# Row fetch for 96 tokens instead of 80, and 17 instead of 10 homes for expert tables

## The chip, the core and the metric

The kernel runs on one core of a Trainium2 chip. The metric is the device time of one execution in microseconds, median over runs. The engines that matter here are TensorE (PE, with its weight loads PEld), VectorE (DVE), ScalarE (ACT), GpSimd (POOL) and the two DMA queues that SyncE (SP) and GpSimd feed. All numbers of the trace come from one profiled execution.

## What is computed

Two transformer blocks on 256 tokens of width 1024. The change is in the last part of the second block, a layer of 16384 experts from which each token uses 128 (8 heads, 16 each):

```python
def peer_ffn(h, w_pq, peer_keys, peer_u, peer_v):
    q = (ht @ w_pq).reshape(T, PEER_HEADS, 2, PEER_HALF)
    sub = jnp.einsum('thpc,hpnc->thpn', q, peer_keys)
    s_top, i_top = lax.top_k(sub, PEER_TOPK)
    ...
    best_s, pos = lax.top_k(cand_s, PEER_TOPK)
    expert = jnp.take_along_axis(cand_i, pos, axis=-1)
    gate = jax.nn.softmax(best_s, axis=-1)
    def chunk(args):
        xc, ec, gc = args
        u = jnp.take(peer_u, ec, axis=0)
        act = jax.nn.gelu(jnp.einsum('cd,ckd->ck', xc, u))
        vv = jnp.take(peer_v, ec, axis=0)
        return jnp.einsum('ck,ckd->cd', gc * act, vv)
```

`peer_u` and `peer_v` are 16384 x 1024 in float32. The result is added to x, which is then normed and stored.

## The kernel before

**Two paths for the expert layer.** The 256 tokens are divided. For the last 176 tokens (N = 256 - TS) the kernel works densely: it multiplies with all 16384 rows of both tables and lets a matrix of gates (zero for experts that were not chosen) select. For the first 80 tokens (TS) it works sparsely: it fetches only the rows that these tokens chose, 128 rows of 4 KB per fetch.

**Dense path.** Each table comes as 128 tiles of 128 x 1024 float32, 512 KB each, by SP's DMA queue (`_dma`, L192). TensorE does 8 matmuls (16 passes in the trace) per tile. First all 128 tiles of u (L1580, then gelu on ACT and a product on DVE, L1598), with 22 batches of gate matmuls between them (`g_batch`, L1536); then all 128 tiles of v (L1659), which add up in four PSUM banks `acc`. The first 24 u tiles (U0) need no gates. The first gate batch needs the top-k of the second half of the tokens, which DVE works out. After the last v tile the sums in `acc` are scaled into `fT`: four of the eight parts on DVE (L1665), four on ACT (L1663).

**Sparse path.** `sparse` fetches with an indirect DMA from GpSimd (L1484) into one of four buffers `ug` (SB = 4). DVE consumes each: a dot product per u row (L1489, 80 of them), then a weighted sum per v row into `sacc` (L1501 and twice L1499, 80 of them). The fetch that uses a buffer again waits for DVE's instruction on it. At the end TensorE adds `sacc` up over partitions (L1676) and DVE scales the result into the sparse columns of `fT` (L1680). Then `back` turns `fT` around (L1650), adds x, norms and stores.

**Homes.** A table tile needs a place in SBUF when its load is issued. Before, ten 4 KB-per-partition places are used in turn: four of the pool `raw`, three each of `whi` and `wlo`. `self.depth` says how many tiles ahead of its use a load may be issued. The tiles of weights that come before the tables (`w_pq` last) use the same queue and the same `raw` places. The tags `bighi` and `biglo` hold `h4`, the input of the routing, which is dead once `hN` and the routing products are made.

**What sets the order.** Each engine takes its instructions from one queue in a fixed order. The program order is `peer()`; a scheduler of the framework reorders it at build time by a simulated time line, so where an instruction stands in its engine's queue follows from that schedule and not from the source alone. The source spreads the steps of `sparse` over the tiles (`step`, SC = 222).

Of the kernel before, what the change touches and what calls it, by code (L numbers as in the profile page):

```python
# [9 lines left out]
F32 = mybir.dt.float32  # L10
# [122 lines left out]
class Kernel:  # L133
# [47 lines left out]
    PRE = (0, 0, 4)  # L181
    DQ = "gpsimd"

    def _dma(self):
        n = self.ndma - self.nwide
        if n < 0 or n % 10 < 4:
            t = self.raw.tile([128, 1024], F32, name="raw")
        elif n % 2 == 0:
            t = self.his.tile([128, 1024], F32, name="raw", tag="whi")
        else:  # L190
            t = self.los.tile([128, 1024], F32, name="raw", tag="wlo")
        self.nc.sync.dma_start(t, self.wspec[self.ndma][0])  # L192
        self.rawt[self.ndma] = t
        self.ndma += 1
# [5 lines left out]

    def _split(self, pin=lambda i: i):
        j = self.nsplit
        while self.ndma < min(len(self.wspec), j + self.depth):
            self._dma()
        t = self.rawt.pop(j)
        flag = self.wspec[j][1]
        if "R" in flag:
            self.wt[j] = t
            self.nsplit += 1
            return  # L210
        if "G" in flag:
            self.nc.gpsimd.tensor_tensor(t, t, self.gt1, OP.mult)
        late = "L" in flag
        hi = (self.late if late else self.his).tile([128, 1024], F32R, name="whi")
        lo = (self.late if late else self.los).tile([128, 1024], F32R, name="wlo")
        i = self.nc.scalar.activation(hi, t, AF.Copy)  # L216
        pin(i)
        if self.fenced:
            self.behind(i, self.fence[0])
        e = self.nc.gpsimd if j in self.POOL_LO or "P" in flag else self.nc.vector  # L220
        i = e.tensor_tensor(lo, t, hi.bitcast(F32), OP.subtract)  # L221
        pin(i)
        if self.fenced:
            self.fenced -= 1
            if e is self.nc.vector:
                self.behind(i, self.fence[1])
        self.wt[j] = (hi, lo)
        self.nsplit += 1
# [1212 lines left out]
                V.tensor_tensor(self.gb[1][:, t0], g, self.gb[0][:, t0], OP.subtract)  # L1441


    TG = ((0, 64), (64, 16))
    TS = 80
    SB = 4

    def rows_init(self, SP):
        nc, V = self.nc, self.nc.vector
        TS, self.SP = self.TS, SP  # L1450
        m = [SP.tile([128, 1024], F32, name="ug", bufs=self.SB) for _ in range(3)]
        for t, i in zip(m, (4, 3)):
            self.dq.dma_start(t[0:TS], self.modd[:, 1024 * i:1024 * i + 1024].to_broadcast([TS, 1024]))
        h = m[2][0:TS]
        V.scalar_tensor_tensor(h, self.x[0:TS, 0], self.r4[0:TS], m[0][0:TS], op0=OP.mult, op1=OP.mult)
        V.tensor_tensor(h, h, m[1][0:TS], OP.add)
        self.hrow, self.pair = [], []
        for t0, n in self.TG:
            r = SP.tile([128, 1024], F32, name=f"hrow{t0}")
# [5 lines left out]
            self.pair.append(p)  # L1465
        self.slot = SP.tile([128, 2, TS], F32, name="slot")
        self.sdot, self.sw = [SP.tile([128, TS], F32, name=n) for n in ("sdot", "sw")]

    def slots(self, e, i, j):
# [4 lines left out]
        V.tensor_copy(ids[0:TS, 1], fl(e)[0:TS])  # L1474
        for t0, n in self.TG:
            for q in range(128 // n):
                self.dq.dma_start(self.slot[n * q:n * q + n, :, t0:t0 + n], ids[t0:t0 + n, :, n * q:n * q + n])

    def sparse(self):
        nc, V, A, G = self.nc, self.nc.vector, self.nc.scalar, self.nc.gpsimd  # L1480

        def fetch(rows, s):
            t = self.SP.tile([128, 1024], F32, name="ug", bufs=self.SB)
            G.indirect_dma_start(t, None, rows, bass.IndirectOffsetOnAxis(self.slot[:, 0, s:s + 1].bitcast(U32), 0))  # L1484
            return t
        slots = [(g, s) for g, (t0, n) in enumerate(self.TG) for s in range(t0, t0 + n)]
        for g, s in slots:
# [6 lines left out]
        for g, s in slots:  # L1494
            t = fetch(self.io["peer_v"].rearrange("a b c -> (a b) c"), s)
            w = self.sw[:, s:s + 1]
            if s == self.TG[g][0]:
                self.sacc.append(self.SP2.tile([128, 1024], F32, name=f"sacc{g}"))
# [50 lines left out]
    def peer(self):  # L1549
        nc, V, A, G, tc = self.nc, self.nc.vector, self.nc.scalar, self.nc.gpsimd, self.tc  # L1550
# [17 lines left out]
        with ExitStack() as st:  # L1568
# [4 lines left out]
            TS, N = self.TS, 256 - self.TS  # L1573
# [3 lines left out]
            def u_dot(ps):  # L1577
                w = self.wget_raw()
                for k in range(8):
                    nc.tensor.matmul(ps, w[:, 128 * k:128 * k + 128], hN[:, k], start=k == 0, stop=k == 7)  # L1580
            A0 = st.enter_context(tc.tile_pool(name="act0", bufs=1))
            act = [A0.tile([128, self.U0, N], F32, name="act0")]
            at = lambda i: act[0][:, i] if i < self.U0 else act[1][:, i - self.U0]

            def u_chunk(i):
                ps = self.psum()
                u_dot(ps[:, 0:N])
                A.activation(at(i), ps[:, 0:N], AF.Gelu_apprx_tanh)

            def u_mul(i, n, U):  # L1590
                ps = self.psum()
                u_dot(ps[:, 0:N])
                w = at(i)
                t = U.tile([128, N], F32, name="ut")
                A.activation(t[:, 0:n], ps[:, 0:n], AF.Gelu_apprx_tanh)  # L1595
                if n < N:
                    A.activation(w[:, n:], ps[:, n:N], AF.Gelu_apprx_tanh)
                V.tensor_tensor(w[:, 0:n], w[:, 0:n], t[:, 0:n], OP.mult)  # L1598
            with tc.tile_pool(name="route", bufs=1) as K:
                R = type("R", (), dict(iota=iota, pool=PT))  # L1600
                with self.ps_pool("prt") as self.prt:
                    subs = self.route(R, K, h)
                with self.ps_pool("ptk") as self.ptk:
                    self.topk(R, K, subs)
                self.depth = 10
                for i in range(self.U0):
                    u_chunk(i)
            self.ls.close()
# [47 lines left out]
            for i in range(128):  # L1656
# [12 lines left out]
                if i == 126:  # L1669
                    for _ in sparse:  # L1670
                        pass
                    for d0 in (0, 4):
                        ps = self.psum()
                        for d in range(4):
                            for g, (t0, n) in enumerate(self.TG):
                                nc.tensor.matmul(ps[:, TS * d + t0:TS * d + t0 + n],  # L1676
# [69 lines left out]
```

## Time and profile before

| | |
|---|---|
| median of 3 runs | 1355.09 us (1353.15 to 1356.93) |
| the profiled execution | 1349.1 us |
| its span in the trace | 1347.3 us |
| PE / PEld busy | 1272.3 us (94%) / 1204.3 us (89%) |
| DVE / ACT / POOL busy | 885.6 us (66%) / 453.7 us (34%) / 457.8 us (34%) |
| moved by DMA | 344.56 MB, mean 256 GB/s |

Spans and rows are of the profiled execution; it was some 6 us faster than the median. Busy shares are means over stages with different limits, so they say little about this change; the stages of the expert layer begin about 690 us into the span.

### The profile page before, as it was taken

The numbers are of one execution on the slowest core, as the hardware profiler recorded it, in microseconds if no ns is written. First come the engines' busy times: TensorE is split into PE (matmuls) and PEld (weight loads), VectorE is DVE, ScalarE is ACT, GpSimd is POOL, SyncE is SP. The second block draws the span as 40 slices with busy tenths as digits, with TensorE's granted clock in tenths as the row PEclk, the third lists the DMA queues.
The fourth block names the chain that finished last, engine by engine and source line by source line (L and its number), as shares of the span: only waits on it lengthen the run. The fifth ranks groups of instructions, "written<-read, shape, count | busy, mean of one in ns | idle before, by whom it ended". The sixth has DMA issues, their size and how long they took to land.

```text
span 1347.3 us, 22547 instructions
## 1 busy us (share of the span) xinstructions
PE 1272.3 (94%) x8682; PEld 1204.3 (89%) x8682; DVE 885.6 (66%) x1790; ACT 453.7 (34%) x917; POOL 457.8 (34%) x384
## 2 busy tenths in 40 slices
PE   6898989999999999986999899999999999999996
PEld 5787869988979888974999899999999999999996
DVE  8995866898669986486779966777655454441003
ACT  4336655666568656534522221111110000000001
POOL 5931022763017643056102443333324333330000
PEclk9897989999999998998999999999999999999999
DMA  5321536888718463436486999999999999998650
GB/s 199 104 85 63 198 128 233 319 304 319 245 48 289 155 237 104 146 117 200 159 279 219 344 376 361 359 378 365 349 357 365 408 409 408 409 409 331 222 200 32
DMA packets 98667, 344.56 MB, mean 256 GB/s; under 512 B 14881, under 2 KB 15009, under 8 KB 98177
## 3 DMA queue, kind: packets, MB, share of 16 engines
q1 hardware_dynamic: 71904, 251.28, 51.4%
q0 software_dynamic: 26368, 91.34, 18.4%
q8 instruction: 68, 1.11, 0.3%
q10 hardware_dynamic: 288, 0.52, 0.1%
q14 instruction: 39, 0.31, 0.1%
HBM read 339.31 MB, written 2.12 MB: 253 GB/s over the span
## 4 chain that ended last, share of the span: by engine, by line
PE 70%; DVE 18%; DMA 4%; issue 3%; ACT 2%; POOL 2%; SPq 1%; ACTq 0%; DVEq 0%; POOLq 0%
PE acc L1659 23%; PE m L1580 18%; PE m L262 14%; DVE wlo L221 4%; PE acc L1091 3%; PE acc L848 2%; PE g L1536 2%; DMA raw<-w_gu 1%; PE pq L1091 1%; POOL adaacc L400 1%; DMA adaw<-w_ada 1%; SPq L649 1%; POOL adaacc L402 1%; PE s L718 1%; DVE work L1323 1%
## 5 line engine op out<-in xcount | busy, mean ns | idle before, releaser
L1580 PE MATMUL m<-hN,raw 128*128 128x176 f32 x2048 | 311.0, 313 | 0.0
L1659 PE MATMUL acc<-act,raw 128*128 128x176 f32 x2048 | 306.4, 313 | 0.0
L1659 PEld LDWEIGHTS acc<-act,raw 128*128 128x128 f32 x2048 | 305.5, 190 | 0.3 <-DVE fT L1665 0.3
L1580 PEld LDWEIGHTS m<-hN,raw 128*128 128x128 f32 x2048 | 305.7, 190 | 0.0
L221 DVE TENSOR_TENSOR wlo<-raw,whi 128x1024 fp32r<-128x1024 f32 x150 | 233.5, 1567 | 66.0 <-ACT whi L216 65.1
L216 ACT ACTIVATE whi<-raw 128x1024 fp32r<-128x1024 f32 x166 | 173.7, 1054 | 134.5 <-PE m L262 60.7
L1501 DVE SCALAR_TENSOR_TENSOR sacc<-ug,sw,sacc 128x1024 f32<-128x1024 f32 x78 | 100.2, 1284 | 100.0 <-DMA ug<-peer_v,slot 99.9
L1484 POOL DMA_INDIRECT ug<-u_rows,slot x80 | 98.9, 1236 | 151.4 <-DVE ug L1489 92.9
L1484 POOL DMA_INDIRECT ug<-peer_v,slot x80 | 77.9, 973 | 134.1 <-DVE sacc L1501 110.7
L262 PE MATMUL m<-h_hi,whi 128*128 128x256 f32 x768 | 115.9, 289 | 4.2 <-ACT h_hi L906 3.0
L262 PE MATMUL m<-h_hi,wlo 128*128 128x256 f32 x768 | 112.8, 286 | 5.3 <-DVE wlo L221 4.7
L262 PE MATMUL m<-h_lo,whi 128*128 128x256 f32 x768 | 114.5, 288 | 2.0 <-DVE h_lo L907 2.0
L262 PEld LDWEIGHTS m<-h_hi,whi 128*128 128x128 f32 x768 | 104.3, 194 | 8.4 <-ACT h_hi L906 3.5
L262 PEld LDWEIGHTS m<-h_hi,wlo 128*128 128x128 f32 x768 | 100.7, 191 | 7.6 <-DVE wlo L221 5.5
L262 PEld LDWEIGHTS m<-h_lo,whi 128*128 128x128 f32 x768 | 103.1, 194 | 3.1 <-DVE h_lo L907 2.4
L1663 ACT ACTIVATE fT<-acc,gt 128x176 f32<-128x176 f32 x4 | 1.5, 406 | 308.3 <-PE acc L1659 308.2
L1489 DVE SCALAR_TENSOR_TENSOR ug<-ug,hrow 128x1024 f32<-128x1024 f32 x80 | 97.1, 1217 | 0.0
L1595 ACT ACTIVATE ut<-m 128x8 f32<-128x8 f32 (+21 forms) x104 | 25.8, 248 | 184.4 <-PE m L1580 177.9
L400 POOL TENSOR_TENSOR adaacc<-adaacc,adaw 128x1024 f32<-128x1024 f32 x24 | 66.0, 2752 | 47.5 <-ACT adaw L399 47.0
L1598 DVE TENSOR_TENSOR act<-act,ut 128x8 f32<-128x8 f32 (+21 forms) x104 | 25.9, 252 | 75.5 <-ACT ut L1595 74.6
L1680 DVE TENSOR_SCALAR fT<-m,gt 128x80 f32<-128x80 f32 x8 | 1.9, 294 | 111.0 <-PE m L1676 111.0
L221 POOL TENSOR_TENSOR wlo<-raw,whi 128x1024 fp32r<-128x1024 f32 x16 | 40.8, 2559 | 22.8 <-ACT whi L216 18.3
(522 smaller groups left out, 1783.9 us busy)
## 6 DMA issues: line engine op xcount, KB each, us to landing
raw<-peer_u SPq DMA_DIRECT2D x128, 512.0 KB
raw<-peer_v SPq DMA_DIRECT2D x128, 512.0 KB
raw<-w_in SPq DMA_DIRECT2D x62, 512.0 KB
adaw<-w_ada SPq DMA_DIRECT2D x48, 512.0 KB
raw<-w_gu SPq DMA_DIRECT2D x44, 512.0 KB
raw<-w_down SPq DMA_DIRECT2D x22, 512.0 KB
raw<-w_out SPq DMA_DIRECT2D x16, 512.0 KB
raw<-w_pq SPq DMA_DIRECT2D x16, 512.0 KB
```

The costliest lines, as they stand in the source:

```text
L216: i = self.nc.scalar.activation(hi, t, AF.Copy)
L221: i = e.tensor_tensor(lo, t, hi.bitcast(F32), OP.subtract)
L262: self.nc.tensor.matmul(out, w(k), x(k), start=start and c == 0, stop=stop and c == last)
L400: G.tensor_tensor(accs[1], accs[1], w, OP.add)
L848: self.nc.tensor.matmul(acc[2 * tt + n], a[:, k, tt * 128:tt * 128 + 128], w[:, 512 * n:512 * n + 512], start=first and (tt, n) not in see ...
L1091: self.nc.tensor.matmul(out, a[:, 2 * c + kk, tt * 128:tt * 128 + 128], w[:, 512 * kk:512 * kk + 512], start=c + i + kk == 0, stop=c == 3 ...
L1484: G.indirect_dma_start(t, None, rows, bass.IndirectOffsetOnAxis(self.slot[:, 0, s:s + 1].bitcast(U32), 0))
L1489: V.scalar_tensor_tensor(t, t, 1.0, self.hrow[g], op0=OP.mult, op1=OP.mult, accum_out=self.sdot[:, s:s + 1])
L1501: V.scalar_tensor_tensor(self.sacc[g], t, w, self.sacc[g], op0=OP.mult, op1=OP.add)
L1536: nc.tensor.matmul(ps[:, t // 4, 128 * (t % 4):128 * (t % 4) + 128], jo[:, t // 2, :, t % 2], io[:, q, t // 2, :, t % 2], start=q == 0, st ...
L1580: nc.tensor.matmul(ps, w[:, 128 * k:128 * k + 128], hN[:, k], start=k == 0, stop=k == 7)
L1659: nc.tensor.matmul(part(d), w[:, 128 * d:128 * d + 128], at(i), start=i == 0 and d % 2 == 0, stop=i == 127, skip_group_check=True)
```

## The change

TS goes from 80 to 96, so the dense path keeps 160 tokens (N = 160) and there are 96 fetches for u and 96 for v; the second group of tokens has 32 tokens and not 16 (`TG`). A new pool `raw2` gives three more homes for tables (RB = 3), and four more are the two halves each of `bighi` and `biglo`, for tables 13 to 16 alone. `home` maps the number of a table tile to its place. The depth is 13 tiles, and 17 while the first 30 table tiles are issued.

```diff
+    RB = 3
+
+    def home(self, n):
+        if 10 + self.RB <= n < 14 + self.RB:
+            n -= 10 + self.RB
+            if n % 2 == 0:
+                self.pairs = self.bt.tile([128, 2, 1024], F32, name="raw2", tag=("bighi", "biglo")[n // 2])
+            return self.pairs[:, n % 2]
+        if n >= 14 + self.RB:
+            n -= 4
+        n = n % (10 + self.RB) if n >= 0 else 0
+        pool, tag = ((self.raw, "raw") if n < 4 else (self.his, "whi") if n < 7 else
+                     (self.los, "wlo") if n < 10 else (self.raw2, "raw2"))
+        return pool.tile([128, 1024], F32, name="raw", tag=tag)
...
-        while self.ndma < min(len(self.wspec), j + self.depth):
+        while self.ndma < len(self.wspec):
+            early = self.depth > self.RAW and self.ndma - self.nwide < 24 + 2 * self.RB
+            if self.ndma >= j + self.depth + (4 if early else 0):
+                break
             self._dma()
...
-    TG = ((0, 64), (64, 16))
-    TS = 80
+    TG = ((0, 64), (64, 32))
+    TS = 96
...
+            self.raw2 = st.enter_context(tc.tile_pool(name="raw2", bufs=self.RB))
...
-                self.depth = 10
+                self.depth = 10 + self.RB
```

Lines after the new code move down by 9 to 13: L192 becomes L201, L1484 L1496, L1489 L1501, L1501 L1513, L1665 L1678, L1676 L1689 and L1680 L1693.

**The end of DVE's queue.** The rows below are DVE's instructions from the last weighted sums of v rows to the last copies into `fT` (`x58` stands for 58 in a row), before:

```order
L1501 SCALAR_TENSOR_TENSOR sacc_10475<-ug,sw,sacc_10475 128x1024 x58
L1499 TENSOR_SCALAR sacc_11548<-ug,sw 128x1024
L1501 SCALAR_TENSOR_TENSOR sacc_11548<-ug,sw,sacc_11548 128x1024 x15
L1680 TENSOR_SCALAR fT<-m,gt_10369 128x80 x8
L1665 TENSOR_SCALAR fT<-acc_10357,gt_10369 128x176
L1665 TENSOR_SCALAR fT<-acc_10358,gt_10369 128x176
L1665 TENSOR_SCALAR fT<-acc_10359,gt_10369 128x176
L1665 TENSOR_SCALAR fT<-acc_10360,gt_10369 128x176
```

The same place in DVE's queue after the change:

```order
L1504 SCALAR_TENSOR_TENSOR sw<-sw,slot 128x96
L1511 TENSOR_SCALAR sacc_10467<-ug,sw 128x1024
L1513 SCALAR_TENSOR_TENSOR sacc_10467<-ug,sw,sacc_10467 128x1024 x50
L1678 TENSOR_SCALAR fT<-acc_10346,gt_10358 128x160
L1678 TENSOR_SCALAR fT<-acc_10347,gt_10358 128x160
L1678 TENSOR_SCALAR fT<-acc_10348,gt_10358 128x160
L1678 TENSOR_SCALAR fT<-acc_10349,gt_10358 128x160
L1513 SCALAR_TENSOR_TENSOR sacc_10467<-ug,sw,sacc_10467 128x1024 x13
L1511 TENSOR_SCALAR sacc_11400<-ug,sw 128x1024
L1513 SCALAR_TENSOR_TENSOR sacc_11400<-ug,sw,sacc_11400 128x1024 x31
L1693 TENSOR_SCALAR fT<-m,gt_10358 128x96 x8
```

The four copies out of `acc`, which need the last v tile's matmuls, stood behind all v rows; now they stand behind 51 of the 96, and 45 v rows stand behind them. Ahead of the rows shown, 17 of the 96 u rows now stand behind the last product of the dense u path; before, none did.

**The end of PE's queue.** These are TensorE's last instructions around L1676 (the sums over partitions of `sacc`), before:

```order
L1659 MATMUL acc_10360<-act_7970,raw 128x176 x2
L1676 MATMUL m<-pair_6768,sacc_10475 128x64
L1676 MATMUL m<-pair_6773,sacc_11548 128x16
...
L1676 MATMUL m<-pair_6773,sacc_11548 128x16
L1659 MATMUL acc_10357<-act_7970,raw 128x176
L1659 MATMUL acc_10358<-act_7970,raw 128x176
```

And after, where L1672 is the v matmul and L1689 the sum over partitions:

```order
L1672 MATMUL acc_10348<-act_7969,raw 128x160
L1672 MATMUL acc_10349<-act_7969,raw 128x160
L1689 MATMUL m<-pair_6768,sacc_10467 128x64 x2
L1689 MATMUL m<-pair_6773,sacc_11400 128x32
...
L1689 MATMUL m<-pair_6773,sacc_11400 128x32
L1663 MATMUL m<-eye,fT 128x128 x16
```

Before, the last v tile's 8 matmuls stood behind the sums over partitions; now all v matmuls stand ahead of them.

**SP's queue at the start of the tables.** These are the loads that SP issues from the store of x (`xd`) to the last table, before:

```order
L1553 DMA xd<-x 128x2048
L192 DMA raw<-w_pq 128x1024 x9
L192 DMA raw<-peer_u 128x1024 x128
L192 DMA raw<-peer_v 128x1024 x128
L1691 DMA out<-xl 128x512 x2
```

And after, where `raw_7703` and `raw_7700` are the places in `bighi` and `biglo`:

```order
L1565 DMA xd<-x 128x2048
L201 DMA raw<-w_pq 128x1024
L201 DMA raw<-peer_u 128x1024 x3
L201 DMA raw<-w_pq 128x1024 x8
L201 DMA raw<-peer_u 128x1024 x9
L201 DMA raw_7703<-peer_u 128x1024
L201 DMA raw<-peer_u 128x1024
L201 DMA raw_7700<-peer_u 128x1024 x2
L201 DMA raw_7703<-peer_u 128x1024
L201 DMA raw<-peer_u 128x1024 x111
L201 DMA raw<-peer_v 128x1024 x128
```

Three table loads now stand ahead of the last eight loads of `w_pq`.

## Rows read from the trace of the kernel before

**Rows 1.** The page: span, PE, and three groups (busy, mean ns, idle before).

```profile
span 1347.3 us, 22547 instructions
...
PE 1272.3 (94%) x8682; PEld 1204.3 (89%) x8682; DVE 885.6 (66%) x1790; ACT 453.7 (34%) x917; POOL 457.8 (34%) x384
...
L1501 DVE SCALAR_TENSOR_TENSOR sacc<-ug,sw,sacc 128x1024 f32<-128x1024 f32 x78 | 100.2, 1284 | 100.0 <-DMA ug<-peer_v,slot 99.9
...
L1489 DVE SCALAR_TENSOR_TENSOR ug<-ug,hrow 128x1024 f32<-128x1024 f32 x80 | 97.1, 1217 | 0.0
...
L1680 DVE TENSOR_SCALAR fT<-m,gt 128x80 f32<-128x80 f32 x8 | 1.9, 294 | 111.0 <-PE m L1676 111.0
```

**Rows 2.** Chain that ended last, from 689 us: start us, us, engine, tile, line.

```profile
689.22 0.44 PE sub L1340 x4
...
761.39 3.57 PE g L1536 x32
...
781.72 0.92 PE g L1536 x16
782.64 9.60 PE m L1580 x64
...
1025.47 303.11 PE acc L1659 x2032
1328.57 3.48 PE m L1676 x32
1332.05 1.29 PE acc L1659 x8
...
1335.17 0.56 PE m L1650 x5
```

**Rows 3.** Windows: us, busy (x) of PE, PEld, DVE, ACT, POOL, PEclk, DMA share, GB/s.

```profile
720.00:740.00 20.00, 19.93 (x135) 19.65 (x134) 20.00 (x93) 3.53 (x11) 7.32 (x12) 1.00 0.65 219
...
1050.00:1100.00 50.00, 50.00 (x337) 50.00 (x336) 24.40 (x19) 0.00 (x0) 18.32 (x20) 1.00 1.03 409
...
1150.00:1200.00 50.00, 50.00 (x338) 50.00 (x337) 23.41 (x19) 0.00 (x0) 18.02 (x19) 1.00 1.03 409
...
1250.00:1300.00 50.00, 50.00 (x337) 50.00 (x336) 0.00 (x0) 0.00 (x0) 0.00 (x0) 1.00 0.65 222
```

**Rows 4.** Time line of GpSimd: start us, us, operation, idle before and its releaser.

```profile
731.93 5.26 POOL L1477 DMA_DIRECT2D slot<-ids  x10 [41.62 <-DVE best L1321]
737.49 1.14 POOL L1484 DMA_INDIRECT ug<-u_rows,slot  x1 [0.30 <-issue]
...
1011.40 0.59 POOL L307 DMA_DIRECT2D gfin<-rows  x1 [9.63 <-PE g L1536]
...
1013.74 1.91 POOL L1484 DMA_INDIRECT ug<-peer_v,slot  x1 [0.79 <-DVE sacc L1499]
...
1207.12 0.95 POOL L1484 DMA_INDIRECT ug<-peer_v,slot  x1 [1.62 <-DVE sacc L1501]
1209.68 0.94 POOL L1484 DMA_INDIRECT ug<-peer_v,slot  x1 [1.61 <-DVE sacc L1501]
```

**Rows 5.** All waits of TensorE from 686 to 1330 us: total, times, longest.

```profile
PE tk L1434 <- DVE sel L1426: 2.5, 2, 2.3
PE tk L1434 <- DVE gexp L1394: 1.5, 2, 1.1
PE g L1536 <- DVE gres L1439: 1.0, 1, 1.0
```

**Rows 6.** Time line of DVE, same columns as rows 4.

```profile
761.05 0.28 DVE L1439 TENSOR_SCALAR gres<-tk 128x128 f32<-128x128 f32 x1
...
1022.55 1.28 DVE L1501 SCALAR_TENSOR_TENSOR sacc<-ug,sw,sacc 128x1024 f32<-128x1024 f32 x1 [1.06 <-DMA ug<-peer_v,slot]
...
1218.90 1.28 DVE L1501 SCALAR_TENSOR_TENSOR sacc<-ug,sw,sacc 128x1024 f32<-128x1024 f32 x1 [1.29 <-DMA ug<-peer_v,slot]
```

**Rows 7.** Time line of SP's DMA issues, merged: start us, us, operation.

```profile
645.77 22.17 SPq L192 DMA_DIRECT2D raw<-w_pq  x8
673.03 327.96 SPq L192 DMA_DIRECT2D raw<-peer_u  x128
```

More of the change, by code (lines that the diff above doesn't have):

```diff
@@ L182 @@
     DQ = "gpsimd"
-    def _dma(self):
[L185 to L191, printed above, removed]
+    RB = 3
[11 more added lines that the diff above has]
+        return pool.tile([128, 1024], F32, name="raw", tag=tag)
+    def _dma(self):
+        t = self.home(self.ndma - self.nwide)
         self.nc.sync.dma_start(t, self.wspec[self.ndma][0])
```

## The prediction

> **What bounds the kernel now.** I read the page first for the span, 1347.3 us [rows 1], and then the chain that ended last. From 761.4 us, where the first gate batch starts, it is TensorE alone, without a gap: 64 passes of the u stage in 9.60 us, a gate batch of 0.92 us, and 2032 passes of the v stage in 303.11 us [rows 2]. That is 150.0 and 149.2 ns a pass of 176 columns, so about 2.39 us a table tile. TensorE waited in all this time only around 761 us, for the top-k on DVE: 5.0 us in three kinds of wait, none on a table [rows 5]. So the dense path sets the end.
>
> The windows say what stands close behind. While v rows are fetched, the DMA engines move 409 GB/s, with share 1.03, in each 50 us; when the fetches are done, 222 GB/s [rows 3]. One fetch is issued every 2.56 us (1207.12 to 1209.68) [rows 4]. A fetch is 128 x 4 KB = 0.524 MB, so fetches take 205 GB/s, and of the 409 the table queue gets the other 204: one tile each 2.56 us, slower than TensorE's 2.39. The ten homes hide this. DVE's last v row starts at 1218.90 us [rows 6], and the 111.0 us of idle ahead of L1680 [rows 1] is the time by which the sparse path was early: the sum over partitions stands ahead of the last tile in TensorE's queue and starts at 1328.57 us [rows 2].
>
> **What the change costs and gives, on paper.** Dense tiles get cheaper. A pass of 128 columns takes 0.44 / 4 = 110 ns [rows 2]; between 110 and 149.2 ns a straight line gives 136 ns for 160 columns, 2.178 us a tile and 0.216 us less than now. Over 256 tiles that would be 55 us, and two gate batches fewer give 1.8 us. The sparse path gets 16 fetches more per table: 32 x 2.56 = 82 us at the present pace, less than the 111 us that it has in hand, but the dense path's end comes nearer by up to 55 us as well. So by amounts of work the two paths would end near each other. The order decides.
>
> **The u stage.** The 27 tiles ahead of the first gate batch gain 27 x 0.216 = 5.8 us, which ends in a longer wait: the batch waits for DVE's `gres`, which ran at 761.05 us [rows 6], and DVE is busy 20.00 of 20 us before it [rows 3]. In DVE's new queue nine u products stand ahead of `gres` and not six, so 3 x 1.22 us [rows 1] = 3.7 us more, if each row has landed. The slots take 6 DMA issues instead of 10 (5.26 us for ten [rows 4]), so rows come about 2 us sooner; bounds 0 and 8 us, taken 4. First batch at about 765.4 us. From there 101 tiles and 20 batches: 101 x 2.178 + 20 x 0.92 + 2 (what the same sum misses today: 101 x 2.39 + 22 x 0.92 = 261.6 against 264.1 us between the two rows) = 240. The v stage starts at about 1006 instead of 1025.5.
>
> The three table loads that now stand ahead of eight `w_pq` loads cost the queue 3 x 1.28 = 3.8 us, where 1.28 is 0.524 MB at 409 GB/s. Those eight loads spread over 22.17 us [rows 7], 2.8 us each, so the queue is not what paces them; I take nothing, at most 3.8 us if the first of them is needed at once. POOL's load of x into `bighi` must now wait until table 14 has been used, and the slots stand behind it. 15 tiles from 690 us on are done by about 723 us, before the slots at 731.93 [rows 4]: nothing.
>
> The homes: at the v stage's start 13 tiles can lie ready. With supply at 2.56 us and use at 2.178, one home is lost per 14.6 us while fetches run, so 13 last about 190 us; the old ten would last 146. The fetches run about 165 us into the v stage (next part). So TensorE isn't starved: 128 x 2.178 = 279 us, and the last v tile ends at about **1285 us**. If no tile lay ready at 1006 us, 165 us would give 64 tiles instead of 76, and the end would come 12 x 2.178 = 26 us later; that is the upper bound.
>
> **The end, where I expect the loss.** In DVE's new queue the four copies out of `acc` stand behind 51 of 96 v rows. They can't run before the last v tile, and 45 v rows stand behind them. An instruction at the head of a queue holds what is behind it: the load of `gfin` on POOL ran only after 9.63 us of waiting for the last gate batch, and the next fetch was issued after it, at 1013.74 [rows 4]. DVE reaches the copies early: 17 u rows and 51 v rows from 1006 us on, four of them already landed, 64 x 2.56 = 164 us, so at about 1170 us. There it stands for 115 us. POOL fetches four rows more, fills the four buffers and stops too. After 1285 us and 0.6 us of copies, 45 v rows follow with nothing beside them. What was hidden work becomes tail.
>
> The price of a row in this tail isn't in the trace, since no fetch ran without tables beside it. From below: DVE's 1.284 us for one [rows 1], 45 x 1.284 = 58 us. From above: the round trip of one buffer as it is now. The last fetch is issued at 1209.68 and used at 1218.90, 9.22 us later [rows 4, 6]; another, issued at 1013.74, was used at 1022.55, 8.81 us [rows 4, 6]. With 1.28 us on DVE and 0.30 us from release to issue [rows 4] that is 10.8 us a round and, with four buffers, 2.7 us a row; at most the present 2.56, or 115 us. Alone on the engines a transfer takes 1.28 instead of 2.56 us, and a fetch has one or two others ahead of it: taking off two to three times 1.28 leaves 8.2 to 7.0 us a round, 2.06 to 1.74 us a row. I take 1.85: 44 x 1.85 + 1.28 = **83 us**.
>
> Here the Trainium skill speaks the other way. "DMA: Bandwidth & Descriptors", section "Anatomy of one DMA — SWDGE (gpsimd) path", fits such a DMA as 2.0 us and bytes / 436e3; an estimate from that page is 3.2 us for 0.524 MB, 4.8 us a round with DVE, 1.2 us a row, under DVE's own time. By the page the tail would be 58 us; the 8.81 and 9.22 us of the trace, even halved, stand nearer to my figure.
>
> Behind the last row: 3.48 us for the sums [rows 2], four copies of 0.294 us [rows 1] = 1.2, about 1 us for the first transposes, which today run beside the last tile, and from 1335.17 us [rows 2] to the end 12.1 us. Together 17.8 us.
>
> **Sum.** 1285 + 0.6 + 83 + 17.8 = 1386.4 against 1347.3 us: 39 us longer. The profiled execution took 1349.1 us, the median 1355.09; 39 us on the median give 1394. I forecast **1392 us**.
>
> **Rivals.**
> A, the forecast: tail at 1.6 to 2.3 us a row.
> B, the tail runs at DVE's pace, 1.284 us a row, with all else as in the sum: 1285 + 0.6 + 58 + 17.8 = 1361.4, 14 us longer, 1369 on the median. For it: four rows lie ready, and DVE had no pause of its own on u rows (idle 0.0) [rows 1]. Against it: the round trips above.
> C, the tables starve TensorE on top of the tail: 1311 instead of 1285 us, so about 1412, or 1420 on the median. For it: 409 GB/s is reached already [rows 3]. Against it: TensorE waits for no table today [rows 5].
> D, the other side: TensorE's passes shrink with the columns much faster than the line, to the 110 ns of the 128-column pass, 1.76 us a tile. Then the dense path would come to the copies close to when DVE does, DVE wouldn't stand, and the end would be set by bytes: from about 750 us some 213 MB (about 215 tiles and 192 fetches) at 409 GB/s, 1271 us, then the last copies and sums, about 1295 us, or 1303 on the median. It decides if the last v tile is done before about 1246 us, where the tail of 101 us no longer passes today's end. Against it: 149.2 and 110 ns go with the columns (0.85 and 0.86 ns a column).
> E, nothing moves, because the extra fetches only fill idle DMA time and the order on DVE doesn't bind: 1355. The `gfin` row speaks against that.
>
> **Chances.** A 0.64, B 0.17, C 0.12, D 0.04, E 0.03. A measurement of this kernel tells changes of about 0.3% (4 us) from none. Slower by more than that: A, B and C, 0.93; within: 0.03; faster: 0.04. A alone spans 1.6 to 2.3 us a row, tails of 72 to 102 us, and 1381 to 1413 us on the median. Reaching down to B's 1369 and up to C's middle, the range is 1368 to 1418.
>
> **What would show it.** Right: DVE idle for over 80 us with PE's v matmul (now L1672) as the releaser of an `acc` copy (L1678); the DMA rate near 240 GB/s while it stands; after the last v tile a stretch of 60 to 110 us in which TensorE is idle, DVE and POOL alternate and 45 rows pass; v passes of about 136 ns; no TensorE wait on a table. Wrong: DVE's weighted sums ending before the last v tile; passes at 149 ns (then the end is 55 us later) or below 120 ns; TensorE waiting for DMA in the v stage.

## The result and the profile after

The changed kernel takes 1406.54 us (median of 4 runs, 1405.94 to 1409.02) against 1356.01 us (1353.15 to 1358.92) for the kernel before: ratio 1.0376, 95% interval 1.0350 to 1.0402. It is slower by about 50 us. The profiled execution took 1405.94 us, its span is 1404.2 us; that is 56.9 us more than the span in [rows 1], since the profiled execution of before was some 7 us quicker than its own median.

The page of the changed kernel, the groups that answer to [rows 1] (busy, mean ns, idle before and its releaser):

```profile
span 1404.2 us, 22615 instructions
...
PE 1236.9 (88%) x8650; PEld 1162.9 (83%) x8650; DVE 917.5 (65%) x1826; ACT 450.3 (32%) x914; POOL 474.2 (34%) x408
...
L1672 PEld LDWEIGHTS acc<-act,raw 128*128 128x128 f32 x2048 | 278.8, 190 | 7.1 <-DMA raw<-peer_v 7.0
...
L1513 DVE SCALAR_TENSOR_TENSOR sacc<-ug,sw,sacc 128x1024 f32<-128x1024 f32 x94 | 120.8, 1285 | 91.9 <-DMA ug<-peer_v,slot 91.4
L1496 POOL DMA_INDIRECT ug<-peer_v,slot x96 | 97.7, 1017 | 232.2 <-DVE sacc L1513 214.9
...
L1689 PE MATMUL m<-pair,sacc 128*128 128x64 f32 (+1 forms) x32 | 7.3, 412 | 81.5 <-DVE sacc L1513 81.5
...
L1678 DVE TENSOR_SCALAR fT<-acc,gt 128x160 f32<-128x160 f32 x4 | 1.3, 377 | 109.7 <-PE acc L1672 109.7
```

Two rows carry the story. The last: four copies of 0.377 us each made DVE wait 109.7 us for TensorE's last v matmul. In [rows 1] DVE idled nearly as long (111.0 us), but at the very end of its work, where only short copies were queued behind. The row above it: TensorE then waited 81.5 us for DVE's weighted sums, which never happened before. TensorE is busy 35 us less than before and the kernel is 57 us longer.

The time line of DVE at that place (start us, us, operation, idle before and its releaser):

```profile
1189.97 1.28 DVE L1513 SCALAR_TENSOR_TENSOR sacc<-ug,sw,sacc 128x1024 f32<-128x1024 f32 x1 [1.27 <-DMA ug<-peer_v,slot]
1300.93 1.26 DVE L1678 TENSOR_SCALAR fT<-acc,gt 128x160 f32<-128x160 f32 x4 [109.68 <-PE acc L1672]
1302.11 5.24 DVE L1513 SCALAR_TENSOR_TENSOR sacc<-ug,sw,sacc 128x1024 f32<-128x1024 f32 x4
1310.04 1.29 DVE L1513 SCALAR_TENSOR_TENSOR sacc<-ug,sw,sacc 128x1024 f32<-128x1024 f32 x1 [2.70 <-DMA ug<-peer_v,slot]
...
1382.71 2.61 DVE L1513 SCALAR_TENSOR_TENSOR sacc<-ug,sw,sacc 128x1024 f32<-128x1024 f32 x2 [0.41 <-DMA ug<-peer_v,slot]
```

The 51st v row starts at 1189.97 us. Then DVE stands. After the copies, four rows run without a pause (5.24 us for four): those are the four buffers that were full. From the fifth row on, DVE waits for each fetch. 45 rows end at 1385.32 us, 83.2 us after the copies, 1.85 us a row. GpSimd's time line shows the other side of the same wait:

```profile
1191.52 0.94 POOL L1496 DMA_INDIRECT ug<-peer_v,slot  x1 [1.62 <-DVE sacc L1513]
...
1305.06 1.78 POOL L1496 DMA_INDIRECT ug<-peer_v,slot  x1 [112.59 <-DVE sacc L1513]
```

The windows cut the last 300 us into stretches (us, busy (x) of PE, PEld, DVE, ACT, POOL, PEclk, DMA share, GB/s):

```profile
1100.00:1150.00 50.00, 50.00 (x369) 49.80 (x368) 24.71 (x20) 0.00 (x0) 17.85 (x19) 1.00 1.03 408
1150.00:1200.00 50.00, 47.76 (x317) 43.17 (x316) 20.55 (x16) 0.00 (x0) 15.97 (x17) 1.00 1.03 408
1200.00:1250.00 50.00, 50.00 (x369) 49.98 (x369) 0.00 (x0) 0.00 (x0) 0.00 (x0) 1.00 0.89 335
1250.00:1300.00 50.00, 50.00 (x371) 50.00 (x370) 0.00 (x0) 0.00 (x0) 0.00 (x0) 1.00 0.39 135
1300.00:1350.00 50.00, 3.87 (x25) 3.47 (x23) 32.76 (x29) 1.26 (x4) 30.00 (x24) 0.56 0.70 232
1350.00:1385.00 35.00, 0.00 (x0) 0.00 (x0) 25.38 (x20) 0.00 (x0) 15.98 (x18) 0.50 0.80 283
```

Read them downwards: both paths at 408 GB/s, as in [rows 3]; then 100 us of TensorE alone, with DVE and GpSimd at 0.00; then 85 us of DVE and GpSimd alone, with TensorE at nearly nothing. What ran side by side in [rows 3] now runs in turn.

Lines of the two dense stages (count: ns min/median/max of one, first and last start us):

```profile
L1592 PE MATMUL m<-hN,raw x2048: 299/299/576, 697.0 to 1016.7; 128*128 128x160 f32 x187
...
L1672 PE MATMUL acc<-act,raw x2048: 299/299/403, 1016.8 to 1302.5; 128*128 128x160 f32 x187
```

TensorE's time line (same columns as DVE's) has the first gate batch and the sums over partitions:

```profile
775.29 3.17 PE L1548 MATMUL g<-io,jo 128*128 128x128 f16 x28 [0.87 <-DVE gres L1451]
...
1385.37 6.18 PE L1689 MATMUL m<-pair,sacc 128*128 128x32 f32 x28 [57.59 <-DVE sacc L1513]
```

### The profile page after: what moved, and what is told of

Its sections match the earlier page's. It is cut to its first block, busy times and chain, and to the rows that moved or that the text cites. A ratio compares the mean times of both kernels' runs of the same rounds, so it can differ in the third digit from the quotient of the medians.

```text
span 1404.2 us, 22615 instructions
## 1 busy us (share of the span) xinstructions
PE 1236.9 (88%) x8650; PEld 1162.9 (83%) x8650; DVE 917.5 (65%) x1826; ACT 450.3 (32%) x914; POOL 474.2 (34%) x408
## 4 chain that ended last, share of the span: by engine, by line
PE 39%; DMA 19%; DVE 18%; issue 16%; POOL 5%; ACT 2%; SPq 0%; DVEq 0%; POOLq 0%; ACTq 0%
PE m L1592 15%; PE m L274 13%; DMA ug<-peer_v,slot 12%; DVE wlo L233 4%; PE acc L1103 3%; DVE sacc L1513 2%; PE acc L860 2%; DMA adaw<-w_ada 2%; POOL ug L1496 2%; DMA raw<-w_gu 1%; PE g L1548 1%; PE pq L1103 1%; ACT whi L228 1%; DMA bias<-bias 1%; DVE adaacc L409 1%
## 5 line engine op out<-in xcount | busy, mean ns | idle before, releaser
L1592 PE MATMUL m<-hN,raw 128*128 128x160 f32 x2048 | 286.4, 301 | 3.4 <-ACT act L1601 3.4
L1672 PE MATMUL acc<-act,raw 128*128 128x160 f32 x2048 | 283.7, 300 | 2.2
L1592 PEld LDWEIGHTS m<-hN,raw 128*128 128x128 f32 x2048 | 281.9, 192 | 3.6 <-ACT act L1601 3.6
L1672 PEld LDWEIGHTS acc<-act,raw 128*128 128x128 f32 x2048 | 278.8, 190 | 7.1 <-DMA raw<-peer_v 7.0
L1513 DVE SCALAR_TENSOR_TENSOR sacc<-ug,sw,sacc 128x1024 f32<-128x1024 f32 x94 | 120.8, 1285 | 91.9 <-DMA ug<-peer_v,slot 91.4
L1496 POOL DMA_INDIRECT ug<-peer_v,slot x96 | 97.7, 1017 | 232.2 <-DVE sacc L1513 214.9
L1496 POOL DMA_INDIRECT ug<-u_rows,slot x96 | 101.0, 1052 | 202.3 <-DVE ug L1501 106.5
L1501 DVE SCALAR_TENSOR_TENSOR ug<-ug,hrow 128x1024 f32<-128x1024 f32 x96 | 117.0, 1220 | 32.1 <-DMA ug<-u_rows,slot 32.0
L412 POOL TENSOR_TENSOR adaacc<-adaacc,adaw 128x1024 f32<-128x1024 f32 x24 | 64.1, 2671 | 50.9 <-ACT adaw L411 50.5
L1676 ACT ACTIVATE fT<-acc,gt 128x160 f32<-128x160 f32 x4 | 1.3, 392 | 242.7 <-PE acc L1672 242.7
L1689 PE MATMUL m<-pair,sacc 128*128 128x64 f32 (+1 forms) x32 | 7.3, 412 | 81.5 <-DVE sacc L1513 81.5
L1608 ACT ACTIVATE ut<-m 128x8 f32<-128x8 f32 (+19 forms) x104 | 25.0, 242 | 160.5 <-PE m L1592 158.1
L1689 PEld LDWEIGHTS m<-pair,sacc 128*128 128x128 f32 x32 | 7.0, 330 | 81.9 <-DVE sacc L1513 57.8
L1678 DVE TENSOR_SCALAR fT<-acc,gt 128x160 f32<-128x160 f32 x4 | 1.3, 377 | 109.7 <-PE acc L1672 109.7
```

The costliest lines, as they stand in the source:

```text
L412: G.tensor_tensor(accs[1], accs[1], w, OP.add)
L1501: V.scalar_tensor_tensor(t, t, 1.0, self.hrow[g], op0=OP.mult, op1=OP.mult, accum_out=self.sdot[:, s:s + 1])
L1513: V.scalar_tensor_tensor(self.sacc[g], t, w, self.sacc[g], op0=OP.mult, op1=OP.add)
L1672: nc.tensor.matmul(part(d), w[:, 128 * d:128 * d + 128], at(i), start=i == 0 and d % 2 == 0, stop=i == 127, skip_group_check=True)
```

## The experiments

Theory: the time is lost to an order, four copies on DVE that wait for TensorE's last tile ahead of 45 rows of the sparse path, and each row behind them costs the round trip of a buffer. Rivals: 96 rows are simply too many for the fetch path, in whatever order; or the homes (later tables, starved tiles) cost it. In one group of runs the kernel before took 1356.68 us (median of 13), in the other 1355.52 us (median of 7); each ratio is against the runs of its own group. Where two kernels are set side by side below, their medians can come from different groups; the kernel before differs by about 1 us between them.

**The copies on another engine.** All eight copies out of `acc` go to ScalarE, which has nothing queued behind them. Work, rows and homes stay.

```diff
-                        if d % 2:
-                            A.activation(F[:, d, TS:], part(d), AF.Copy, scale=gt[:, d:d + 1])
-                        else:
-                            V.tensor_scalar(F[:, d, TS:], part(d), gt[:, d:d + 1], None, op0=OP.mult)
+                        A.activation(F[:, d, TS:], part(d), AF.Copy, scale=gt[:, d:d + 1])
```

> The change with all eight copies out of acc on ACT, so that DVE's queue holds no instruction that waits for the last v tile; nothing else differs. My theory (the copies' place in DVE's queue costs the time): DVE isn't held, the 45 rows behind the copies run beside the v tiles at 2.56 us each and end at about 1306 us into the span instead of 1385; TensorE runs out of ready tables near 1206 us and then goes at the queue's pace, last v tile at about 1315, median about 1335 us, 21 us faster than before. Rival 1 (sixteen tokens more are simply too many rows for the DMA engines, whatever the order): within 5 us of the change, 1402 to 1411. Rival 2 (the order costs, but with it mended DMA eats the gain): 1350 to 1362, like before.

Measured: 1334.30 us (1330.08 to 1335.69), ratio 0.9832 (0.9803 to 0.9860). 72 us off the changed kernel, and 22 us under the kernel before. The last v row now starts beside the last tiles, not behind them (time line of DVE):

```profile
1307.58 1.28 DVE L1513 SCALAR_TENSOR_TENSOR sacc<-ug,sw,sacc 128x1024 f32<-128x1024 f32 x1 [1.27 <-DMA ug<-peer_v,slot]
```

**The copies on DVE, tied behind the last v row.** The same instructions on the same engines; the tie changes their place in DVE's queue. With it the scheduler also put the sums over partitions ahead of the last v matmuls again; with the copies on ScalarE they stay behind them, and the gain is there as well.

```diff
-                V.scalar_tensor_tensor(self.sacc[g], t, w, self.sacc[g], op0=OP.mult, op1=OP.add)
+                self.lastv = V.scalar_tensor_tensor(self.sacc[g], t, w, self.sacc[g], op0=OP.mult, op1=OP.add)
...
-                            V.tensor_scalar(F[:, d, TS:], part(d), gt[:, d:d + 1], None, op0=OP.mult)
+                            self.behind(V.tensor_scalar(F[:, d, TS:], part(d), gt[:, d:d + 1], None, op0=OP.mult), self.lastv)
```

> The change with its four DVE copies out of acc kept on DVE, but tied by a pure order dependency behind the last v row. The same amount of work on the same engines as in the change. My theory: as with the copies on ACT, and 2 us less because the sums over partitions again stand ahead of the last v tile: about 1333 us. Rival 1: within 5 us of the change, 1402 to 1411. A rival by which it is DVE's load and not the order (the ACT variant gains, this one doesn't): 1390 or more.

Measured: 1330.66 us (1327.19 to 1332.73), ratio 0.9807 (0.9780 to 0.9834). The time line of DVE: the wait for `acc` is now 6.52 us and at the end.

```profile
1305.26 1.28 DVE L1513 SCALAR_TENSOR_TENSOR sacc<-ug,sw,sacc 128x1024 f32<-128x1024 f32 x1 [1.25 <-DMA ug<-peer_v,slot]
...
1313.07 1.26 DVE L1678 TENSOR_SCALAR fT<-acc,gt 128x160 f32<-128x160 f32 x4 [6.52 <-PE acc L1672]
```

Its line of v matmuls, and its windows to the end of the fetches:

```profile
L1672 PE MATMUL acc<-act,raw x2048: 299/299/403, 1012.5 to 1318.3; 128*128 128x160 f32 x187
```

```profile
800.00:1000.00 200.00, 200.00 (x1625) 199.35 (x1624) 133.81 (x292) 39.23 (x186) 58.06 (x58) 1.00 0.99 373
...
1200.00:1300.00 100.00, 94.42 (x627) 85.85 (x626) 48.28 (x38) 0.00 (x0) 34.80 (x38) 1.00 1.03 409
```

The group of its v weight loads, with its wait for tables:

```profile
L1672 PEld LDWEIGHTS acc<-act,raw 128*128 128x128 f32 x2048 | 279.9, 190 | 22.4 <-DMA raw<-peer_v 21.1
```

Both runs settle the first rival: 96 rows are not too many, the same rows and tables end 76 us sooner in another order. They show a price too. With fetches beside it to the end, the v stage takes 305.8 us; 3.65 of these are the sums over partitions, which stand inside it again, so the v tiles take 302 us instead of 285.7. The rate stays at 409 GB/s, the tables get half of it, and TensorE's weight loads wait 21.1 us for them. That is 2.36 us a tile, nearly the 2.39 of before the change [rows 2]: most of what the shorter passes gained over before lies in the u stage (692.5 to 1012.5 us, 320.0, against 336.0 before).

**The homes alone.** The changed kernel with 80 tokens; two extra homes in `raw2`, since three don't fit beside the wider tiles.

```diff
-    RB = 3
+    RB = 2
...
-    TG = ((0, 64), (64, 32))
-    TS = 96
+    TG = ((0, 64), (64, 16))
+    TS = 80
```

> The homes alone: 80 tokens on the row fetch as before, with two homes in the new pool instead of three (three don't fit beside 80) and the four in the idle routing input, depth 12 and 16. The copies stand behind all 80 v rows, as before. My theory: TensorE waited for no table before, so more homes give nothing: 1356 within 3 us. Rival (the early table loads ahead of eight w_pq loads and the load of x behind table 14 delay the routing): 3 to 8 us slower. Rival (homes give what the DMA engines' idle time holds): 5 us or more faster.

Measured: 1353.50 us (median of 10, 1350.65 to 1359.52), ratio 0.9983 (0.9965 to 1.0001): the homes alone are worth nothing that stands clear of the noise, in either direction.

**The rows alone.** The kernel before with 96 tokens and its ten homes.

```diff
-    TG = ((0, 64), (64, 16))
-    TS = 80
+    TG = ((0, 64), (64, 32))
+    TS = 96
```

> The tokens alone: 96 tokens with the ten homes and the depth of before. Here 48 v rows stand ahead of the four copies on DVE and 48 behind them. My theory: the same held queue, three rows more in the tail at 1.8 us (5 us), and ten homes instead of 13 run out within the fetch, so the last v tile comes 3 to 8 us later: 1413 to 1422, and a tail of 48 rows in 85 to 92 us. Rival (the loss comes from the homes: their loads collide with w_pq or with the fetches): near 1340. Rival (homes matter nothing): 1406 to 1412, by the three rows alone.

Measured: 1411.50 us (1408.56 to 1415.99), ratio 1.0420 (1.0385 to 1.0456), just below what I expected, so that the total alone doesn't separate it from "homes matter nothing". The trace does. Its time line of DVE has the same wait, here with 48 rows behind it:

```profile
1298.23 1.26 DVE L1665 TENSOR_SCALAR fT<-acc,gt 128x160 f32<-128x160 f32 x4 [122.45 <-PE acc L1659]
...
1387.50 1.28 DVE L1501 SCALAR_TENSOR_TENSOR sacc<-ug,sw,sacc 128x1024 f32<-128x1024 f32 x1 [1.11 <-DMA ug<-peer_v,slot]
```

48 rows end 89.3 us after the copies: 1.86 us a row, the same price. And the group of its v weight loads, with its wait for tables:

```profile
L1659 PEld LDWEIGHTS acc<-act,raw 128*128 128x128 f32 x2048 | 279.2, 190 | 12.0 <-DMA raw<-peer_v 11.9
```

11.9 us against 7.0 with the homes; the v stage runs from 1008.8 to 1299.8 us, 291.0 us, 5.3 longer. So the whole loss comes with the rows. The homes take some 5 us off the v stage in these two traces; the 5 us between the two medians have overlapping intervals.

**Six buffers instead of four.** Is the price of a row in the tail the round trip of a buffer, or DVE's own pace? Two homes pay for the space.

```diff
-    RB = 3
+    RB = 1
...
-    SB = 4
+    SB = 6
```

> The change with six buffers ug for fetched rows instead of four, and one home in the new pool instead of three to make room; the copies stay where the scheduler puts them: 57 v rows ahead, 38 behind. My theory: in the tail a row costs the round trip of a buffer divided by the number of buffers. 83.2 us for 45 rows is 1.85 us, a round trip of 7.4 us; with six that would be 1.23, so DVE's own 1.285 sets the pace: 38 rows in 49 to 52 us. Rival (1.85 us is the pace of GpSimd's issue or of the DMA engines on single rows, not of the buffers): 38 rows in 68 to 72 us.

Measured: 1374.87 us (1372.54 and 1377.20), ratio 1.0140 (1.0092 to 1.0189). Its copies stand behind 57 rows, one row stands between them, and 38 follow, from 1301.8 to 1356.6 us (time line of DVE):

```profile
1301.77 7.88 DVE L1513 SCALAR_TENSOR_TENSOR sacc<-ug,sw,sacc 128x1024 f32<-128x1024 f32 x6
...
1353.98 2.61 DVE L1513 SCALAR_TENSOR_TENSOR sacc<-ug,sw,sacc 128x1024 f32<-128x1024 f32 x2 [0.65 <-DMA ug<-peer_v,slot]
```

54.7 us is 1.44 us a row: better than 1.85, so buffers did set the price, but not DVE's 1.285. GpSimd's time line shows that behind the first two fetches no release by DVE is waited for any more:

```profile
1327.12 1.01 POOL L1496 DMA_INDIRECT ug<-peer_v,slot  x1 [0.31 <-issue]
1328.43 1.02 POOL L1496 DMA_INDIRECT ug<-peer_v,slot  x1 [0.30 <-issue]
...
1332.39 1.70 POOL L1496 DMA_INDIRECT ug<-peer_v,slot  x1 [0.31 <-issue]
```

Its window for most of that tail:

```profile
1310.00:1355.00 45.00, 0.88 (x4) 0.69 (x4) 38.59 (x31) 0.00 (x0) 31.91 (x28) 0.50 0.95 349
```

One issue after another, most of them 1.01 or 1.02 us, some up to 1.96, with 0.30 us between them: GpSimd goes from fetch to fetch without a free moment. The rival had named GpSimd's issue or the DMA engines as the pace, but at 1.85 us; neither theory had 1.44. Whether the issue itself is the next limit isn't shown: the DMA engines are near full too (share 0.95, 349 GB/s, against 1.03 and 409 beside the tables), and no run tells an issue that is long by itself from one that waits for them. Of the 31.7 us off the changed kernel, seven rows fewer in the tail account for 7 x 1.85 = 13 and the price for 38 x 0.41 = 16.

**The right order with ten homes.** The kernel with the rows alone, and its copies tied as above (the same two lines).

> The tokens alone (96, ten homes, as before the change), with the four copies tied behind the last v row. Beside the pinned change (1330.7 us) it prices the homes where they can matter. My theory: with the order mended the DMA engines are full from 800 us on, so what is loaded before the fetches start comes off the end: 3 tiles to 7 tiles of 0.524 MB at 409 GB/s, 4 to 9 us slower, 1335 to 1340. Rival (homes still give nothing): 1328 to 1333. Rival (homes were needed against starving, each tile late costs 2.56 us): 1341 to 1349.

Measured: 1335.58 us (1334.36 to 1337.63), ratio 0.9850 (0.9815 to 0.9885). That is 5 us above the tied copies with 13 homes, as expected, but the intervals (0.9780 to 0.9834 there) overlap. The group of its v weight loads shows the direction:

```profile
L1659 PEld LDWEIGHTS acc<-act,raw 128*128 128x128 f32 x2048 | 281.2, 190 | 27.4 <-DMA raw<-peer_v 26.9 <-DVE sacc L1501 0.3
```

26.9 us of waiting for tables against 21.1 with 13 homes; the v stage takes 312.2 us instead of 305.8.

**The first u products behind `gres`.** Tied copies, and the first twelve products of the sparse path tied behind the top-k's last step, to undo the later first gate batch.

```diff
-                V.tensor_scalar(g, ps[:, 0:128], GSCALE, None, op0=OP.mult)
+                self.gres = V.tensor_scalar(g, ps[:, 0:128], GSCALE, None, op0=OP.mult)
...
-            V.scalar_tensor_tensor(t, t, 1.0, self.hrow[g], op0=OP.mult, op1=OP.mult, accum_out=self.sdot[:, s:s + 1])
+            i = V.scalar_tensor_tensor(t, t, 1.0, self.hrow[g], op0=OP.mult, op1=OP.mult, accum_out=self.sdot[:, s:s + 1])
+            if s < 12:
+                self.behind(i, self.gres)
```

> The pinned change with the first twelve u products also tied behind the top-k's last scaling (gres), so that the first gate batch is not late. My theory: the first gate batch starts about 6 us sooner after the dense u stage begins (72 instead of 78 us), but the DMA engines set the end, and the fetches stand still with four full buffers for some 10 us longer; of the 6 us some 0 to 4 are left, 1326 to 1332. Rival (TensorE's start sets the end): 1323 to 1326. Rival (late fetches cost more than they give): 1334 or more.

Measured: 1331.66 us (1329.92 to 1337.23), ratio 0.9817 (0.9784 to 0.9851), the same as without it. The first gate batch comes 65.7 us after the first u pass instead of 78.6 us, but then TensorE waits elsewhere (its time line):

```profile
775.32 1.86 PE L1550 MATMUL g<-io,jo 128*128 128x128 f16 x16 [8.02 <-ACT act L1561]
```

8.02 of the 12.9 us are given back at once, and the u stage gets only 2.4 us shorter (317.6 against 320.0). The window 1200 to 1300 us of this kernel also runs at 409 GB/s.

**88 tokens.** Tied copies, three groups of tokens, one extra home in `raw2`.

```diff
-    RB = 3
+    RB = 1
...
-    TG = ((0, 64), (64, 32))
-    TS = 96
+    TG = ((0, 64), (64, 16), (80, 8))
+    TS = 88
```

> 88 tokens on the row fetch, copies tied behind the last v row, one home in the new pool (more don't fit beside a third group of tokens) and the four in the routing input. My theory: between 80 (TensorE sets the end) and 96 (DMA sets it) the sum is nearly flat: DMA has 16 fetches less, 20 us; TensorE 256 tiles by 0.108 us more, 28 us, of which about 24 us fill the time that it now waits for tables: 1327 to 1335. Rival (rows are the cheaper path at any number): 1340 or more, halfway to 80 tokens. Rival (tables are): 1320 or less.

Measured: 1328.52 us (1325.74 to 1332.17), ratio 0.9807 (0.9772 to 0.9843): the same as 96 tokens. Its window at the end shows a part of the reserve back, fetches done early and TensorE nearly always busy (its weight loads still wait 10.8 us for tables over the v stage, against 21.1 with 96):

```profile
1200.00:1300.00 100.00, 99.69 (x657) 93.66 (x656) 31.05 (x25) 0.00 (x0) 20.59 (x22) 1.00 0.85 337
```

So the two numbers of tokens cost the same. That time is flat between them isn't shown: only these two were run in the right order, and this one has two homes fewer as well. This kernel and the one with tied copies are the fastest of the study, about 26 us under the kernel before and 76 under the changed one.

## Why the prediction was right, and which terms were off

The direction, the mechanism and the place were right: rival A's tail is what happened, and tying those four copies behind the last v row takes 76 us away. One of my proofs of it was none: the fetch behind the `gfin` row was released last by DVE's first v row (0.79 us [rows 4]), with all four buffers full, so that row doesn't show a queue held by its head. The 109.7 us of DVE and the 112.59 us of GpSimd above do. The forecast of 1392 us was 14.5 us low, inside the range; the sum gave 1394 on the median, and no row stood behind the 2 us that I took off. Step by step, on the spans (1386.4 forecast, 1404.2 measured, 17.8 us to account for):

- **The tail.** 83 us forecast, 83.2 measured, 1.85 us a row both times. The six buffers show that the round of a buffer sets this price. That the size met to 0.2 us is in part luck: my working left 1.74 to 2.06 us a row, 78 to 92 us, and 1.85 was a choice within it. Here the Trainium skill ("DMA: Bandwidth & Descriptors", section "Anatomy of one DMA — SWDGE (gpsimd) path") would have given 58 us. The trace does not agree: four buffers at 1.85 us are a round of 7.4 us, where the estimate from the Trainium skill was 4.8. My ground for preferring my figure was weak, though: halved, 8.81 and 9.22 us are 4.4 and 4.6, midway between that 3.2 us and the 5.8 us of mine (7.4 less 1.28 and 0.30). With six buffers the row still cost 1.44 us. Rival B, DVE's pace, is out.
- **A dense tile.** 80 passes of the u stage take 10.92 us in the chain, 136.5 ns each; the straight line gave 136. Rival D is out. Rival E is out as well.
- **The v stage, mis-sized by 5.7 us.** From its start to the end of DVE's copies 285.3 us, where I had 279 and 0.6. I let 13 homes last 190 us. But a home with a load under way is no tile. TensorE first waited for a table at 1149.48 us, 133 us into the stage; in that time it uses 133 / 2.18 = 61 tiles and the queue brings 133 / 2.56 = 52, so about 9 had landed at the start. The kernel with tied copies and ten homes says the same: there the weight loads ran 89.30 us and 41 tiles without a pause, the queue brings 35 in that time, so 6 had landed, again four fewer than homes. TensorE's weight loads show the wait, from an unbroken stretch into one pause a tile (time line):

```profile
1119.89 29.39 PEld L1672 LDWEIGHTS acc<-act,raw 128*128 128x128 f32 x216
1149.48 2.20 PEld L1672 LDWEIGHTS acc<-act,raw 128*128 128x128 f32 x16 [0.20 <-DMA raw<-peer_v]
...
1190.43 2.20 PEld L1672 LDWEIGHTS acc<-act,raw 128*128 128x128 f32 x16 [0.36 <-DMA raw<-peer_v]
```

  The same in the kernel with tied copies and ten homes:

```profile
1009.20 89.30 PEld L1659 LDWEIGHTS acc<-act,raw 128*128 128x128 f32 x656
1098.82 2.20 PEld L1659 LDWEIGHTS acc<-act,raw 128*128 128x128 f32 x16 [0.32 <-DMA raw<-peer_v]
```

  The fetches ran 174 us into the stage and not 164, which drew the waits out. This is a small piece of rival C, 7.0 of its 26 us. It also ended by itself: once DVE stood and the fetches stopped, the tables had the DMA engines alone (335 GB/s in the window from 1200 us), so the loss of the one path was cut by the standstill of the other.
- **The first gate batch, mis-sized by 2.4 us.** 78.3 us after the first u pass instead of 71.9 before: 6.4 us later, where I took 4 of 0 to 8. With 80 tokens and the homes it is 71.9 again, with the rows alone 76.0. So 4.1 us come with the rows and the nine products ahead of `gres`, as I took them; the other 2.3 come only with homes and rows together. I had said "if each row has landed", and the first hadn't: DVE waits 2.54 us for it, against 0.68 with the rows alone, which is about the difference (time line of DVE):

```profile
753.19 1.23 DVE L1501 SCALAR_TENSOR_TENSOR ug<-ug,hrow 128x1024 f32<-128x1024 f32 x1 [2.54 <-DMA ug<-u_rows,slot]
```

  In the right order, the kernel with the first products tied behind `gres` shows that all this was worth next to nothing for the end.
- **From the first gate batch to the v stage.** 241.5 us, 240 forecast; with my rounding of the start (1005.4 to 1006), 0.9 us.
- **Behind the last row, mis-sized by 1.1 us.** 18.9 us instead of 17.8: the granted clock was 0.50, the lower of TensorE's two levels (1.2 GHz), after it had idled through the tail, and 28 of the sums took 6.18 us, where [rows 2] has 3.48 for 32 and the kernel with tied copies, at a granted clock of 1.00, takes 3.65 for the same 32.
- **The start of the dense path, not the change's: 7.5 us.** The first u pass came at 697.0 instead of 689.5 us. The chain was already 9.4 us later at the load of `w_out` (611.78 against 602.39 us), ahead of anything that the change moves; in the eight kernels of the experiments, one trace each, the first u pass lies anywhere from 684.6 to 699.6 us. Across the place where three tables now stand ahead of `w_pq` the lag fell rather than grew, so nothing speaks against costing that at nothing.

7.5 + 2.4 + 0.9 + 5.7 + 0.2 + 1.1 make 17.8. The quick profile of before matters here too: I put its 39 us on the median, and the measured 50.5 us between medians are 56.9 between the profiled executions, 7.5 of them the scatter above.

What stays open: the worth of the extra homes in the right order (5 us between two kernels, with overlapping intervals), and what makes the start of the u stage scatter.

## What to carry to other kernels

When a change shifts work between paths, read each engine's queue for an instruction that waits for another engine's last result, and count what stands behind it: a copy of 0.4 us can hold back 83 us of work, and the same wait costs nothing at the end of the queue. Count as buffer ahead only what has landed, not places with loads under way. Before you credit one path with cheaper work, look whether the other takes the bandwidth: here the v tiles cost 2.36 us again, nearly the old 2.39, as soon as the fetches ran beside them to the end.

## What the hardware showed that I had not expected

With buffers to spare, GpSimd issued indirect fetches back to back, most of them 1.01 or 1.02 us and some up to 1.96, 0.30 us between two; a row cost 1.44 us over 38 rows, more than DVE's 1.285 for one. The end of the kernel behind the idle stretch of TensorE runs at the lower clock (0.50 granted from 1350 to 1391.5 us), and 28 sums over partitions took 6.18 us there, against 3.65 us for the same 32 at a granted clock of 1.00 in the kernel with tied copies.
